# Three transformer-like blocks in one kernel: one mask in the attention, gates in other tiles, pinned table loads, kept weights fetched earlier, and copies of u on VectorE

## The chip, the core and the metric

The kernel runs on one core of a Trainium2 chip. The metric is the device time of one execution in microseconds, as the median of several runs. Five engines work side by side, each through its own list of instructions in order: TensorE (PE, matmuls and transposes), VectorE (DVE), ScalarE (ACT), GpSimd (POOL) and SyncE (SP), which here only issues DMAs. ACT issues DMAs too. An instruction that waits holds back all that stands behind it on its engine.

## The reference

Input is x of 512 tokens by 1024 channels in float32. Two hybrid layers run first, then one second block and a last RMS norm. Cut to what matters:

```
def hybrid_layer(x, ...):                      # twice
    h = rmsnorm(x, pre_mix_g)
    proj = h @ w_in                            # dn q,k,v,z,b,a; sw q,k,v; gate_a, gate_b
    y_a = deltanet_branch(...) @ w_up_dn       # causal conv, gated delta rule, norm * silu(z)
    y_b = swa_sink_branch(...) @ w_up_sw       # window 128, 16 query heads on 2 kv heads
    mix = (sigmoid(gate_a) * y_a + sigmoid(gate_b) * y_b) @ w_o
    x = x + rmsnorm(mix, post_mix_g)
    ff = square(relu(rmsnorm(x, pre_mlp_g) @ w_ff1)) @ w_ff2
    return x + rmsnorm(ff, post_mlp_g)

def second_block(x, ...):                      # once
    ua, za, ub, zb, ga, gb = split(rmsnorm(x) @ w_in_2 + b_in_2)
    # s5: dt = exp(log_dt); mag = exp(lam_re*dt); ang = lam_im*dt; bbar from b_re, b_im
    #     s_t = abar * s_(t-1) + bbar @ u_t ;  y = Re(c @ s) + d*u ; gelu, glu
    ya, yb = s5(ua) * silu(za), pool(ub) * silu(zb)
    return rmsnorm(x + (sigmoid(ga)*(ya@w_a) + sigmoid(gb)*(yb@w_b)) @ w_out)
```

In the attention a block of 128 queries sees its own block of keys and the block before it, and of each 128 of the 256 keys: those at or below the diagonal in its own block, those above it in the block before.

## The kernel before, in words

Activations lie with 128 channels on the partitions and the 512 tokens in the free dimension, so 1024 channels are eight tiles. A float32 matrix product is made of three matmuls in a rounded format: each operand is split into a high part (`xh`, `wh`) and a rest (`xl`, `wl`), and a `dense` block of 128 output channels is 8 x 3 = 24 matmuls of 128x512; `dense_half` is the same for 256 tokens. Weights come by `load_w` (L225 to L243) or by the class `Weights` (L183 to L222): SP loads a 512 KB `raw` tile, ACT casts it to the high part (L241, L221), DVE makes the rest (L242, L222). There are two `raw` tiles, three each of `wh` and `wl`, and one or two more (`rawx`, `raws`) in some stages. A tile is loaded again only when the rest of the weight in it has been made. A scheduler orders the instructions of each engine from the program; what goes through `tc.keep_in_program_order` keeps its place among its like. PSUM has 3 accumulators for the dense blocks (`psm`) and 5 others (`psa`).

The stages of a layer that the change touches, and those around them:

- **Attention.** `sw_item` (L928 to L1026) handles one block `b` of 128 queries and one of the two kv heads, 8 items a layer, beside other work. ACT makes the exponentials (L995), PE transposes the normed scores, ACT copies them to `pc` (L1007), and GpSimd cuts them: `pv` (L1010) keeps what belongs to the block before, `pc` (L1012, in place) what belongs to the own block. Then PE multiplies `pv` with the values of the block before and `pc` with those of the own block.
- **Mix stage** (L1299 to L1365). For each of eight blocks n: SP fetches `ogf` (delta-rule output) and its gate (`gate(0, n)`), DVE multiplies them (L1335), ACT and DVE split the product into `ah` parts (L336, L339), PE does the `dense` block of `w_up_sw`, and DVE multiplies the result with `gate(2, n)` (L1340). `ogf` and both gates come through `fetch` (L1313), which has three tiles (`fe`). A second loop multiplies all eight `ah` with `w_up_dn`.
- **Feed-forward stage** (L1367 to L1510). The first six blocks of `w_ff1` are done in two halves of the tokens with kept weights (`kw`); meanwhile the residual of the mix stage is finished (`rt` L432 on DVE, `xd_mid` to and from DRAM by SP, `xsl` L342). Beside it `ssm_tables` (L1047 to L1175) computes half of the tables of the second block in each layer. It loads small inputs: `row` (8x128), `dt` (64x8x1, two), `lbr`, `lbi` (64x8x16, two each), `crow` (128x2x64, four). `next(tables, None)` advances it by a step per block. The last product with `w_ff2` is done in two halves: three weights from `Weights`, then five kept ones by `load_w` (L1487). The inputs are `hh`, `hl` (relu, square, split: L1380, L1382, L336, L339); `halves3` works on the first three weights at once and leaves the last two inputs to the end.
- **State-space stage** of the second block (from L1558). `tz` tiles are read from DRAM by 32 small DMAs (L1572), 16 issued by ACT and 16 by SP. u is transposed by PE in eight groups, copied to `uab` (L1585, ACT), transposed again and copied to `u_g` (L1592, DVE), and multiplied with `e` and `tz`; ACT copies the products with `e` to `xv` (L1607).

Of the kernel before, what the change touches and what calls it, by code (L numbers as in the profile page):

```python
# [19 lines left out]
P = 128  # L20
# [34 lines left out]
def body(  # L55
# [44 lines left out]
    def rest(n):  # L100
        for _ in range(n):
            yield
# [119 lines left out]
            V.tensor_tensor(out=lo, in0=t, in1=f32(h), op=ALU.subtract)  # L222
            return h, lo

    def load_w(src, kn=KD, n=P, pool_h=False, keep=None):  # L225
        turn[0] += 1
        if turn[0] % 3 == 2 and turn[1] is not None and turn[0] > turn[2]:
            raw = turn[1].tile([P, kn, n], F32, tag="rawx", name="rawx", bufs=1)
        else:
            raw = wp.tile([P, kn, n], F32, tag="raw", name="raw", bufs=2)  # L230
        DMA.dma_start(out=raw, in_=src.rearrange("(k p) n -> p k n", p=P))
        h = lo = None
        if keep is not None:
            h, lo = keep(kn, n), keep(kn, n)
        if h is None:
            h = wp.tile([P, kn, n], F32R, tag="wh", name="wh", bufs=3)
            lo = wp.tile([P, kn, n], F32R, tag="wl", name="wl", bufs=3)
        if pool_h:
            G.tensor_scalar(out=h, in0=raw, scalar1=1.0, scalar2=0.0, op0=ALU.mult, op1=ALU.add)  # L239
        else:  # L240
            S.copy(out=h, in_=raw)  # L241
        V.tensor_tensor(out=lo, in0=raw, in1=f32(h), op=ALU.subtract)  # L242
        return h, lo  # L243

# [682 lines left out]
    def sw_item(l, b, kv, qk, vt, sw, kts, db):  # L927
# [70 lines left out]
        V.reciprocal(out=den, in_=den)  # L998
        V.tensor_tensor(out=sc, in0=sc, in1=den.unsqueeze(3).to_broadcast([P, 2, 4, P]), op=ALU.mult)
        yield from rest(PRB)  # L1000
        pcs = []
        for o in range(2):
            ps = ps_ax()
            for i in range(4):
                T.transpose(ps[:, i, :], sc[:, o, i, :], ident)
            pc, pv = sw.tile([P, 4, P], F32, tag="pc", name="pc", bufs=2), None
            S.copy(out=pc, in_=ps)  # L1007
            if b:
                pv = sw.tile([P, 4, P], F32, tag="pv", name="pv", bufs=2)
                G.affine_select(out=pv, in_=pc, pattern=[[0, 4], [-1, P]], base=0, channel_multiplier=1,  # L1010
                                compare_op=ALU.is_gt, fill=0.0)
            G.affine_select(out=pc, in_=pc, pattern=[[0, 4], [1, P]], base=0, channel_multiplier=-1,  # L1012
                            compare_op=ALU.is_ge, fill=0.0)
            pcs.append((pc, pv))
        yield from rest(PV)
        po = ps_ax()
        for o, (pc, pv) in enumerate(pcs):
            hs = slice(64 * o, 64 * o + 64)
            dst = po[hs].rearrange("p h t -> p (h t)")
            if b:  # L1020
                T.matmul(dst, lhsT=vt[:, b - 1, kv * 64:kv * 64 + 64], rhs=pv.rearrange("p h t -> p (h t)"), start=True, stop=False)
            T.matmul(dst, lhsT=vt[:, b, kv * 64:kv * 64 + 64], rhs=pc.rearrange("p h t -> p (h t)"), start=not b, stop=True)
        of = r2("sof")
        V.tensor_copy(out=of, in_=po)
        DMA.dma_start(out=db[:, 4 * kv:4 * kv + 4, b * P:(b + 1) * P], in_=of)
# [20 lines left out]
    def ssm_tables(sp, hf):  # L1046
# [6 lines left out]

        prs = slice(NG * hf, NG * hf + NG)
        grs = slice(2 * NG * hf, 2 * NG * hf + 2 * NG)
        lam = {}
        for nm, src in (("lr", ssm_lam_re_2), ("li", ssm_lam_im_2)):
            row = sp.tile([NG, P], F32, tag="row", name="row")
            DMA.dma_start(out=row, in_=src[0, grs].rearrange("(i two) p -> i (two p)", two=2))
            ps = ps_ax((P, NG))  # L1060
            T.transpose(ps, row, ident[:NG, :NG])
            lam[nm] = tl(nm)
            V.tensor_copy(out=lam[nm], in_=ps)
        lr, li = lam["lr"], lam["li"]
        dt = tl("dt")
        for half in range(2):
            DMA.dma_start(out=dt[64 * half:64 * half + 64, :],
                          in_=ssm_log_dt_2[0, grs].rearrange("(i two) -> two i", two=2)[half].partition_broadcast(64))
        bre, bim = tl("lbr", (P, NG, 2, 16))[:, :, 0, :], tl("lbi", (P, NG, 2, 16))[:, :, 0, :]
        for dst, src in ((bre, ssm_b_re_2), (bim, ssm_b_im_2)):  # L1070
            for half in range(2):
                DMA.dma_start(out=dst[64 * half:64 * half + 64],
                              in_=src[0, grs].rearrange("(i two) p c -> two p i c", two=2)[half])
        yield

# [26 lines left out]
        for src in (ssm_c_re_2, ssm_c_im_2):  # L1102
            crow = sp.tile([P, 2, 2, 64], F32, tag="crow", name="crow", bufs=2)
            for dup in range(2):
                DMA.dma_start(out=crow[:, :, dup, :], in_=src[0, grs].rearrange("(q g) c p -> (g c) q p", q=2))
            crows.append(crow)
        s16 = (P, NG, 16)
        tC, tD = tl("tC", s16), tl("tD", s16)
# [83 lines left out]
    def layer(l, st, nxt):  # L1192
# [111 lines left out]
        with sbuf(f"mx{l}") as mp:  # L1304
# [11 lines left out]
                return t  # L1316

            def gate(i, n):
                t = fetch(dg[i], n, "gate")
                if (i, n) in plain:  # L1320
                    S.activation(out=t, in_=t, func=gate_fn[i])
                return t
# [47 lines left out]
        with sbuf(f"ff{l}") as ff, ExitStack() as es2:  # L1370
# [109 lines left out]
            for i in range(2):  # L1480
                fs = Stats(tr)
                for n in range(KD):
                    if i == 0 and n == 0:
                        wk = {j: w.take() for j in range(3)}
                        head = halves3([wk[j] for j in range(3)], i)
                    elif i == 0 and n >= 3:
                        wk[n] = load_w(down(3, n)[0], keep=keep)  # L1487
                    ps = head[n] if i == 0 and n < 3 else dense_half(wk[n], hid, i)
                    ac = acc[n][:, HALVES[i]]
                    V.tensor_tensor(out=ac, in0=ps, in1=ac, op=ALU.add)  # L1490
                    fs.add(ac)
                    if i:
                        tick()

                def ff_rstd(i=i, fs=fs):
                    fm = small((P, 2), "fm")
                    V.scalar_tensor_tensor(out=fm, in0=fs.sums(), scalar=1.0 / D, in1=rs4[i], op0=ALU.mult, op1=ALU.mult)
                    V.tensor_scalar(out=fm, in0=fm, scalar1=EPS, scalar2=None, op0=ALU.add)
                    fr = power(fm, 2)
                    V.tensor_tensor(out=fr, in0=fr, in1=rs2[i], op=ALU.mult)  # L1500
                    return fr

                pending = residual(mid, acc, ff_rstd, "post_mlp", l * KD, xst, i)
                if i == 0:
                    before = pending
                    tick = ticks(before, AT_D)
# [52 lines left out]
    with sbuf("ss") as sp:  # L1559
# [20 lines left out]
        for c in range(4):  # L1580
            for j4 in range(2):
                ps = ps_ax((64, 4, P))
                for j in range(4):
                    T.transpose(ps[:, j, :], ua[:, c, 4 * j4 + j::8], ident)
                S.copy(out=uag[:, 8 * c:8 * c + 8, 4 * j4:4 * j4 + 4, :], in_=ps.rearrange("p j (g c) -> p g j c", c=16))  # L1585
        u_g = k8("u_g").rearrange("p a b -> p (a b)").rearrange("p (g b) -> p g b", g=32)
        for g8 in range(4):
            ps = ps_ax((P, 8, 64))
# [180 lines left out]
```

## Time and profile before

| | |
|---|---|
| Median of 3 runs | 2309.17 us (2308.73 to 2314.07) |
| The profiled execution | 2315.69 us, span of the trace 2313.9 us |
| Mean granted clock of TensorE | 0.982 |
| PE busy | 2243.0 us (97%) |
| DVE busy | 1485.3 us (64%) |
| ACT busy | 952.1 us (41%) |
| POOL busy | 609.4 us (26%) |
| DMA | 284.33 MB, 42% of the 16 engines' time on the main queue |

The granted clock has two levels: 1.0 is 2.4 GHz and 0.5 is 1.2 GHz. A mean between them tells which part of a stretch ran at the lower one. In the timeline a time in brackets is how long the engine sat idle before the row, and the arrow says what ended it. A row with xN stands for N like instructions; its second column is the time from the first one's start to the last one's end. SPq and ACTq are the DMA-issuing lists of SP and ACT.

### The profile page before, as it was taken

Reading aid. Unit: us, or ns where it says so; the run is one execution under the profiler, and the core shown is the slowest. Engines: PE = TensorE matmul, PEld = TensorE weight load, DVE = VectorE, ACT = ScalarE, POOL = GpSimd, SP = SyncE. Lnnn points to the kernel's source line nnn. Section 1 sums busy time; section 2 is a strip of 40 time slices with the busy share of each in tenths; the row PEclk is TensorE's granted clock in tenths of the full one; section 3 lists DMA queues with packets and bytes.
Section 4 is the critical chain, followed back from the end, with each engine's and each line's share of the span. In section 5 each row is a group of like instructions: output and inputs, shape, how many; then the busy total and the mean of one; then the engine's idle time right before and its main releaser. Section 6 shows DMA issues by size and latency. Waiting matters only on the chain. (4 is left out here: it accounts for less than half of the span.)

```text
span 2313.9 us, 37654 instructions
## 1 busy us (share of the span) xinstructions
PE 2243.0 (97%) x14460; PEld 1954.5 (84%) x14460; DVE 1485.3 (64%) x2958; ACT 952.1 (41%) x1726; POOL 609.4 (26%) x675
## 2 busy tenths in 40 slices
PE   8999999999999999999999999999999999899998
PEld 7867888887989899988678888889898898877788
DVE  5579793445576777665797934465777775435645
ACT  4554333333464354444533333334643444423333
POOL 1643420200336123246333202003351242200001
PEclk9999999999999999999999999999999999999999
DMA  5223424565453433342233345654434334563344
GB/s 177 62 72 87 101 83 128 172 200 160 121 157 92 128 107 98 116 125 58 77 87 88 92 127 182 201 164 126 136 101 118 114 97 123 169 165 117 108 131 146
DMA packets 466431, 284.33 MB, mean 123 GB/s; under 512 B 48502, under 2 KB 440012, under 8 KB 465740
## 3 DMA queue, kind: packets, MB, share of 16 engines
q1 hardware_dynamic: 462544, 280.69, 41.9%
q8 instruction: 114, 1.87, 0.3%
q10 hardware_dynamic: 3708, 1.24, 0.3%
q14 instruction: 65, 0.53, 0.1%
HBM read 235.76 MB, written 46.11 MB: 122 GB/s over the span
## 5 line engine op out<-in xcount | busy, mean ns | idle before, releaser
L78 PE MATMUL psm<-xsh,wh 128*128 128x512 f32 (+1 forms) x1136 | 445.6, 393 | 2.6 <-ACT wh L241 1.6
L78 PE MATMUL psm<-xsl,wh 128*128 128x512 f32 (+1 forms) x1136 | 432.6, 381 | 8.2 <-DVE xsl L342 4.2
L78 PE MATMUL psm<-xsh,wl 128*128 128x512 f32 (+1 forms) x1136 | 431.6, 380 | 0.0
L242 DVE TENSOR_TENSOR wl<-raw,wh 128x1024 fp32r<-128x1024 f32 (+2 forms) x179 | 213.3, 1192 | 89.9 <-ACT wh L241 63.6
L78 PEld LDWEIGHTS psm<-xsh,wh 128*128 128x128 f32 x1136 | 217.6, 192 | 48.4 <-issue 8.6
L78 PEld LDWEIGHTS psm<-xsl,wh 128*128 128x128 f32 x1136 | 218.1, 192 | 45.9 <-DVE xsl L342 5.5
L78 PEld LDWEIGHTS psm<-xsh,wl 128*128 128x128 f32 x1136 | 217.3, 191 | 40.9
L241 ACT CAST wh<-raw 128x1024 fp32r<-128x1024 f32 (+3 forms) x126 | 123.4, 980 | 253.6 <-PE psm L78 218.2
L370 POOL TENSOR_TENSOR sa<-sa,sq 128x256 f32<-128x256 f32 x54 | 51.5, 955 | 665.8 <-ACT sq L365 381.5
L78 PE MATMUL psm<-hh,wh 128*128 128x512 f32 (+1 forms) x480 | 177.1, 375 | 6.4 <-ACT hh L336 6.4
L78 PE MATMUL psm<-hl,wh 128*128 128x512 f32 (+1 forms) x480 | 177.7, 372 | 0.8 <-DVE hl L339 0.8
L78 PE MATMUL psm<-hh,wl 128*128 128x512 f32 (+1 forms) x480 | 176.7, 370 | 0.0
L221 ACT CAST wh<-raw 128x1024 fp32r<-128x1024 f32 x67 | 70.2, 1050 | 127.4 <-PE psm L78 76.2
L221 ACT CAST wh<-raws 128x1024 fp32r<-128x1024 f32 x63 | 66.0, 1047 | 127.9 <-PE psm L78 93.7
L222 DVE TENSOR_TENSOR wl<-raw,wh 128x1024 fp32r<-128x1024 f32 x67 | 97.4, 1454 | 26.0 <-ACT wh L221 23.5
L78 PEld LDWEIGHTS psm<-hh,wh 128*128 128x128 f32 x480 | 90.5, 191 | 22.8 <-ACT hh L336 7.0
L78 PEld LDWEIGHTS psm<-hl,wh 128*128 128x128 f32 x480 | 91.5, 191 | 16.4 <-DVE hl L339 1.3
L78 PEld LDWEIGHTS psm<-hh,wl 128*128 128x128 f32 x480 | 91.6, 191 | 15.1
L222 DVE TENSOR_TENSOR wl<-raws,wh 128x1024 fp32r<-128x1024 f32 x63 | 93.6, 1486 | 13.2 <-ACT wh L221 13.2
L239 POOL TENSOR_SCALAR wh<-raw 128x1024 fp32r<-128x1024 f32 (+1 forms) x53 | 62.9, 1186 | 121.0 <-PE psm L78 104.0
L78 PE MATMUL psm<-ah,wh 128*128 128x512 f32 x256 | 83.0, 405 | 5.2 <-ACT ah L336 5.0
L78 PE MATMUL psa<-xsh,wh 128*128 128x256 f32 x288 | 82.3, 286 | 0.0
(670 smaller groups left out, 5662.5 us busy)
## 6 DMA issues: line engine op xcount, KB each, us to landing
raw<-in_w_in_dram SPq DMA_DIRECT2D x130, 512.0 KB, 3.9
raw<-in_w_ff_dram SPq DMA_DIRECT2D x75, 512.0 KB, 4.1
raws<-in_w_ff_dram SPq DMA_DIRECT2D x51, 512.0 KB, 4.3
gate<-dg SPq DMA_DIRECT2D x48, 256.0 KB, 4.4
rawx<-in_w_in_dram SPq DMA_DIRECT2D x14, 512.0 KB, 4.1
raw<-in_w_up_sw_dram SPq DMA_DIRECT2D x12, 512.0 KB, 5.0
raw<-in_w_up_dn_dram SPq DMA_DIRECT2D x11, 512.0 KB, 4.5
raw<-in_w_o_dram SPq DMA_DIRECT2D x10, 512.0 KB, 4.7
```

Source lines behind the costliest of these rows:

```text
L78: return s.issue(nc.tensor.matmul(*a, **k))
L221: S.copy(out=h, in_=t)
L222: V.tensor_tensor(out=lo, in0=t, in1=f32(h), op=ALU.subtract)
L239: G.tensor_scalar(out=h, in0=raw, scalar1=1.0, scalar2=0.0, op0=ALU.mult, op1=ALU.add)
L241: S.copy(out=h, in_=raw)
L242: V.tensor_tensor(out=lo, in0=raw, in1=f32(h), op=ALU.subtract)
L370: (G if s.n in POOL_ACC else V).tensor_tensor(out=s.acc, in0=s.acc, in1=sq, op=ALU.add)
```

## The change

Five edits, in the order of the diff:

1. In the state of a kept weight, `load_w` can pin its ACT cast to program order (`pin=True`), used for two weights of the last product with `w_ff2`. These two (3 and 4) are loaded before `halves3`, and weight n + 4 is loaded in step n, so weights stand three to four blocks ahead.
2. In the attention `pc` is no longer cut. The sum p_prev v_prev + p_own v_own is formed as pc v_prev + (pc cut to the own block) (v_own - v_prev): GpSimd makes one cut (`pv`, now with the pattern of the own block), DVE makes `vd`, the difference of the values. For block 0 `pc` is used as it is.
3. The loads of `ssm_tables` go through `queue`, which pins them.
4. `gate(2, n)` goes to a `t2` tile (there are four) instead of one of the three `fe` tiles.
5. The copies to `uab` are made by DVE.

```diff
@@ load_w
-    def load_w(src, kn=KD, n=P, pool_h=False, keep=None):
+    def load_w(src, kn=KD, n=P, pool_h=False, keep=None, pin=False):
...
-            S.copy(out=h, in_=raw)
+            i = S.copy(out=h, in_=raw)
+            if pin:
+                tc.keep_in_program_order(i)
@@ sw_item
+        if b:
+            vd = sw.tile([P, 64], F32, tag="vd", name="vd", bufs=2)
+            V.tensor_tensor(out=vd, in0=vt[:, b, kv * 64:kv * 64 + 64], in1=vt[:, b - 1, kv * 64:kv * 64 + 64], op=ALU.subtract)
...
-                G.affine_select(out=pv, in_=pc, pattern=[[0, 4], [-1, P]], base=0, channel_multiplier=1,
-                                compare_op=ALU.is_gt, fill=0.0)
-            G.affine_select(out=pc, in_=pc, pattern=[[0, 4], [1, P]], base=0, channel_multiplier=-1,
-                            compare_op=ALU.is_ge, fill=0.0)
+                G.affine_select(out=pv, in_=pc, pattern=[[0, 4], [1, P]], base=0, channel_multiplier=-1,
+                                compare_op=ALU.is_ge, fill=0.0)
...
-                T.matmul(dst, lhsT=vt[:, b - 1, ...], rhs=pv..., start=True, stop=False)
-            T.matmul(dst, lhsT=vt[:, b, ...], rhs=pc..., start=not b, stop=True)
+                T.matmul(dst, lhsT=vt[:, b - 1, vs], rhs=pr, start=True, stop=False)
+                T.matmul(dst, lhsT=vd, rhs=pv.rearrange("p h t -> p (h t)"), start=False, stop=True)
+            else:
+                T.matmul(dst, lhsT=vt[:, b, vs], rhs=pr, start=True, stop=True)
@@ ssm_tables (row, dt, lbr, lbi and crow alike)
+        def queue(**k):
+            tc.keep_in_program_order(DMA.dma_start(**k))
...
-            DMA.dma_start(out=row, in_=src[0, grs].rearrange("(i two) p -> i (two p)", two=2))
+            queue(out=row, in_=src[0, grs].rearrange("(i two) p -> i (two p)", two=2))
@@ mix stage
             def gate(i, n):
-                t = fetch(dg[i], n, "gate")
+                if i == 2:
+                    t = t2("gate2")
+                    DMA.dma_start(out=t, in_=dg[i][:, n, :])
+                else:
+                    t = fetch(dg[i], n, "gate")
@@ feed-forward stage, last product
                         wk = {j: w.take() for j in range(3)}
+                        for j in (3, 4):
+                            wk[j] = load_w(down(3, j)[0], keep=keep, pin=True)
                         head = halves3([wk[j] for j in range(3)], i)
-                    elif i == 0 and n >= 3:
-                        wk[n] = load_w(down(3, n)[0], keep=keep)
+                    elif i == 0 and n + 4 < KD:
+                        wk[n + 4] = load_w(down(3, n + 4)[0], keep=keep)
@@ state-space stage
-                S.copy(out=uag[:, 8 * c:8 * c + 8, 4 * j4:4 * j4 + 4, :], in_=ps.rearrange("p j (g c) -> p g j c", c=16))
+                V.tensor_copy(out=uag[:, 8 * c:8 * c + 8, 4 * j4:4 * j4 + 4, :], in_=ps.rearrange("p j (g c) -> p g j c", c=16))
```

The edits also move instructions that the diff doesn't name, because the scheduler makes its order anew. Line numbers are those of each kernel: what was L1059, L1067, L1072 and L1105 (loads of the tables) is L1064 now, and 2 to 16 lines are added to later ones.

On SP, in the first layer's feed-forward stage, the loads of the tables stood in the middle of the residual's traffic before (`raw` are weights, `xd_mid` and `xo` the residual):

```order
L1059 DMA row<-in_ssm_lam_re_dram 8x128
L1067 DMA dt<-in_ssm_log_dt_dram 64x8x1 x2
L1072 DMA lbr<-in_ssm_b_re_dram 64x8x16
L231 DMA raw<-in_w_ff_dram 128x8x128
L1072 DMA lbr<-in_ssm_b_re_dram 64x8x16
L1072 DMA lbi<-in_ssm_b_im_dram 64x8x16
L189 DMA raw<-in_w_ff_dram 128x8x128
L1072 DMA lbi<-in_ssm_b_im_dram 64x8x16
L1105 DMA crow<-in_ssm_c_re_dram 128x2x64 x2
L1105 DMA crow<-in_ssm_c_im_dram 128x2x64 x2
L401 DMA xd_mid_5569<-rt 128x256
L430 DMA xo<-xd_in 128x256
```

Now the residual's traffic stands first and the four `crow` loads behind it, directly ahead of these rows; `tsa` and `tsb` are reads of the finished residual:

```order
L189 DMA raws<-in_w_ff_dram 128x8x128 x2
L1064 DMA row<-in_ssm_lam_re_dram 8x128
L189 DMA raw<-in_w_ff_dram 128x8x128 x3
L321 DMA tsa<-xd_mid_5565 128x512
L321 DMA tsb<-xd_mid_5565 128x512
L321 DMA tsa<-xd_mid_5565 128x512
L321 DMA tsb<-xd_mid_5565 128x512
L1064 DMA row<-in_ssm_lam_im_dram 8x128
L1064 DMA dt<-in_ssm_log_dt_dram 64x8x1 x2
L1064 DMA lbr<-in_ssm_b_re_dram 64x8x16 x2
L1064 DMA lbi<-in_ssm_b_im_dram 64x8x16 x2
L189 DMA raws<-in_w_ff_dram 128x8x128 x2
```

The small loads `dt`, `lbr` and `lbi` moved from the front of the stage, where three weight loads and the residual stood among and behind them, to a place behind five more weight loads and four of `tsa` and `tsb`; two `raws` weights stand directly behind them.

On ACT, at the first layer's last product with `w_ff2`, before (`kw` are casts of kept weights, `ft`, `fq` and `hh` make the last two inputs, `sa` and `sq` are squares for the norm):

```order
L241 CAST kw<-raw 128x1024 x2
L241 CAST kw<-rawx 128x1024
L1380 ACTIVATE ft<-y_9597 128x512
L1382 ACTIVATE fq<-ft 128x512
L336 CAST hh<-fq 128x512
L1380 ACTIVATE ft<-y_9596 128x512
L241 CAST kw<-raw 128x1024
L1382 ACTIVATE fq<-ft 128x512
L336 CAST hh<-fq 128x512
L241 CAST kw<-raw 128x1024
L365 ACTIVATE sa<-acc 128x256
L365 ACTIVATE sq<-acc 128x256 x7
```

And now:

```order
L1394 ACTIVATE ft<-y_9593 128x512
L1396 ACTIVATE fq<-ft 128x512
L1394 ACTIVATE ft<-y_9592 128x512
L338 CAST hh<-fq 128x512
L1396 ACTIVATE fq<-ft 128x512
L338 CAST hh<-fq 128x512
L241 CAST kw<-raw 128x1024 x2
L241 CAST kw<-rawx 128x1024
L367 ACTIVATE sa<-acc 128x256
L367 ACTIVATE sq<-acc 128x256 x2
L241 CAST kw<-raw 128x1024
L367 ACTIVATE sq<-acc 128x256
```

The casts of the kept weights moved behind the last `hh`. In the second layer they do so too.

On ACT, at the state-space stage, before (`za` and `p2t` are other outputs, `wh` casts of weights):

```order
L1552 ACTIVATE za<-psm,prm 128x256 x4
L1572 DMA tz<-hpad 16x8x128 x16
L1585 COPY uab<-psa 64x8x64 x5
L1535 ACT_TABLE_LOAD
L1535 ACTIVATE p2t<-psm,prm 128x512 x2
L241 CAST wh<-rawx 128x1024
L241 CAST wh<-raw 128x1024 x2
L1535 ACTIVATE p2t<-psm,prm 128x512
L1585 COPY uab<-psa 64x8x64 x3
L241 CAST wh<-rawx 128x1024
L1607 COPY xv<-psa 128x512
```

And now:

```order
L1568 ACTIVATE za<-psm,prm 128x256 x4
L1588 DMA tz<-hpad 16x8x128 x16
L1623 COPY xv<-psa 128x512 x2
L1551 ACT_TABLE_LOAD
L1551 ACTIVATE p2t<-psm,prm 128x512
L241 CAST wh<-rawx 128x1024
L1623 COPY xv<-psa 128x512 x2
L241 CAST wh<-raw 128x1024
L1551 ACTIVATE p2t<-psm,prm 128x512
L241 CAST wh<-raw 128x1024
L1551 ACTIVATE p2t<-psm,prm 128x512
```

The copies to `uab` are gone from ACT (they stand on DVE, ahead of its copy to `m8t`), and the first two copies to `xv` come directly behind the sixteen `tz` issues. On PE three dense blocks stood between the fifth and the sixth of the eight groups of u before. Now the sixth to eighth group and the second transposes stand among the first dense block, and the products with `e` and with the first `tz` tile directly behind it. Four matmuls of the second dense block later come the products with the second `tz` tile.

## Rows read from the trace of the kernel before

**Rows 1.** Waits of PE, whole span: for whom, us in total, times, longest

```profile
PE psm L78 <- ACT hh L336: 6.4, 2, 4.4
PE psa L78 <- POOL pv L1010: 6.3, 2, 3.2
PE psm L78 <- ACT ft L1380: 5.4, 2, 2.7
PE psm L78 <- ACT ah L336: 5.0, 2, 2.8
```

**Rows 2.** Windows: stretch, length, busy us and count of each engine, granted clock, DMA

```profile
125.00:145.00 20.00, 16.72 (x85) 11.05 (x83) 9.14 (x16) 13.35 (x45) 6.57 (x7) 0.91 0.17 47
1100.00:1130.00 30.00, 26.86 (x136) 19.88 (x136) 18.71 (x48) 16.52 (x50) 10.61 (x12) 0.89 0.25 71
500.00:540.00 40.00, 36.58 (x146) 29.08 (x145) 20.85 (x27) 10.58 (x13) 0.00 (x0) 0.91 0.65 197
1490.00:1520.00 30.00, 27.56 (x113) 21.87 (x112) 16.82 (x21) 8.06 (x10) 0.00 (x0) 0.94 0.69 208
620.00:660.00 40.00, 33.98 (x250) 32.95 (x250) 22.88 (x40) 22.01 (x52) 12.94 (x15) 0.91 0.62 163
1600.00:1640.00 40.00, 35.76 (x257) 34.95 (x256) 21.79 (x42) 22.41 (x53) 11.75 (x14) 0.87 0.65 171
936.00:956.00 20.00, 17.04 (x116) 16.13 (x115) 12.62 (x20) 10.40 (x16) 0.73 (x1) 0.83 0.49 141
1912.00:1932.00 20.00, 15.00 (x106) 14.30 (x105) 12.98 (x20) 11.11 (x16) 1.20 (x1) 0.83 0.55 159
2044.00:2064.00 20.00, 15.36 (x70) 11.73 (x69) 5.46 (x7) 9.90 (x15) 0.00 (x0) 0.83 0.77 168
```

**Rows 3.** Timeline of ACT, attention: start, length, row, idle before and its releaser

```profile
128.15 1.28 ACT L995 ACT_TABLE_LOAD   x1
...
132.64 1.04 ACT L1007 COPY pc<-psa 128x512 f32<-128x512 f32 x2
```

**Rows 4.** Timeline of DVE, mix stage of the first layer

```profile
499.89 0.75 DVE L1335 SCALAR_TENSOR_TENSOR ogf<-ogf,prm,gate 128x512 f32<-128x512 f32 x1 [4.48 <-DMA gate<-dg]
...
527.84 0.75 DVE L1335 SCALAR_TENSOR_TENSOR ogf<-ogf,prm,gate 128x512 f32<-128x512 f32 x1 [1.94 <-DMA gate<-dg]
```

**Rows 5.** Timeline of SP, feed-forward stage of the first layer

```profile
617.77 1.37 SPq L1067 DMA_DIRECT2D dt<-in_ssm_log_dt_dram  x2
...
621.31 0.41 SPq L231 DMA_DIRECT2D raw<-in_w_ff_dram  x1
...
630.59 2.85 SPq L1072 DMA_DIRECT2D lbi<-in_ssm_b_im_dram  x1
...
669.88 0.31 SPq L1059 DMA_DIRECT2D row<-in_ssm_lam_im_dram  x1
```

**Rows 6.** Timeline of ACT, same stage

```profile
633.02 1.04 ACT L241 CAST kw<-raw 128x1024 fp32r<-128x1024 f32 x1 [10.42 <-DMA raw<-in_w_ff_dram]
```

**Rows 7.** Line L1072, loads of lbr and lbi

```profile
DMA to landing us min/median/max: 7.9/9.7/11.5
```

**Rows 8.** Timeline of DVE, later in that stage

```profile
684.50 0.28 DVE L1030 TENSOR_TENSOR A<-cor,lbr 128x128 f32<-128x128 f32 x1
```

**Rows 9.** Timeline of ACT, last product with w_ff2, first layer

```profile
943.95 1.04 ACT L241 CAST kw<-raw 128x1024 fp32r<-128x1024 f32 x1 [1.26 <-DMA raw<-in_w_ff_dram]
```

**Rows 10.** Timeline of PE, state-space stage

```profile
2043.00 0.39 PE L78 MATMUL psm<-xsh,wh 128*128 128x512 f32 x1
...
2048.21 0.39 PE L78 MATMUL psm<-xsh,wl 128*128 128x512 f32 x1
...
2068.13 3.02 PE L78 MATMUL psa<-u_g,e 128*64 128x64 f32 x96
```

**Rows 11.** Timeline of ACT, state-space stage

```profile
2030.10 20.78 ACTq L1572 DMA_DIRECT2D tz<-hpad  x16
```

**Rows 12.** Tile tz, its loads

```profile
DMA to landing us min/median/max: 2.4/4.1/7.9
```

More of the change, by code (lines that the diff above doesn't have):

```diff
@@ L1019, in sw_item @@
             dst = po[hs].rearrange("p h t -> p (h t)")
+            pr = pc.rearrange("p h t -> p (h t)")
+            vs = slice(kv * 64, kv * 64 + 64)
             if b:
-                T.matmul(dst, lhsT=vt[:, b - 1, kv * 64:kv * 64 + 64], rhs=pv.rearrange("p h t -> p (h t)"), start=True, stop=False)
-            T.matmul(dst, lhsT=vt[:, b, kv * 64:kv * 64 + 64], rhs=pc.rearrange("p h t -> p (h t)"), start=not b, stop=True)
+                T.matmul(dst, lhsT=vt[:, b - 1, vs], rhs=pr, start=True, stop=False)
+                T.matmul(dst, lhsT=vd, rhs=pv.rearrange("p h t -> p (h t)"), start=False, stop=True)
+            else:
+                T.matmul(dst, lhsT=vt[:, b, vs], rhs=pr, start=True, stop=True)
         of = r2("sof")
@@ L1066, in ssm_tables @@
         for half in range(2):
-            DMA.dma_start(out=dt[64 * half:64 * half + 64, :],
+            queue(out=dt[64 * half:64 * half + 64, :],
                           in_=ssm_log_dt_2[0, grs].rearrange("(i two) -> two i", two=2)[half].partition_broadcast(64))
@@ L1071, in ssm_tables @@
             for half in range(2):
-                DMA.dma_start(out=dst[64 * half:64 * half + 64],
+                queue(out=dst[64 * half:64 * half + 64],
                               in_=src[0, grs].rearrange("(i two) p c -> two p i c", two=2)[half])
@@ L1104, in ssm_tables @@
             for dup in range(2):
-                DMA.dma_start(out=crow[:, :, dup, :], in_=src[0, grs].rearrange("(q g) c p -> (g c) q p", q=2))
+                queue(out=crow[:, :, dup, :], in_=src[0, grs].rearrange("(q g) c p -> (g c) q p", q=2))
             crows.append(crow)
```

## Prediction, written before the changed kernel ran

> **What bounds the kernel now.** I read the page first: PE works nearly all the span and no other engine comes near it, so only time in which PE stands still, or runs at the lower clock, can be won. The waits of PE come next. Four releasers that the change touches head its list together with residual work that it doesn't: the last `hh` parts, the cut `pv`, `ft` behind a late kept weight, and `ah` [rows 1]. Each comes twice or so, once a layer. Then I took the windows around these places for the price [rows 2]. A window shows two losses: idle time, which is its length less the busy time of PE, and the clock. At 1.2 GHz a matmul takes twice as long, so half of a stretch at that level is lost; with a mean clock c the loss is (1 - c) times the length. The reader is to see that the clock costs about as much as the waits that come before it. In us, idle and clock: attention 3.3 + 1.8 and 3.1 + 3.3; mix stage 3.4 + 3.6 and 2.4 + 1.8; start of the feed-forward stage 6.0 + 3.6 and 4.2 + 5.2; its last product 3.0 + 3.4 and 5.0 + 3.4; state-space stage 4.6 + 3.4. That is 11.5, 11.2, 19.0, 14.8 and 8.0, in all 64.5 us. More than that the change can't win, for other idle time is elsewhere.
>
> **One mask.** In the attention PE waits for the cuts of GpSimd, but these only wait for ACT: both copies to `pc` stand behind a table load and eight exponentials, from 128.15 to 132.64 [rows 3]. After the change PE's first product needs the uncut copy alone, and the first copy now stands ahead of the table load, so 4.5 us earlier; its cut is made while the exponentials run. The second copy still stands behind them, half a microsecond later than the exponentials did before, so PE still waits for it and then for its cut, which I put at 1 to 2 us a layer. What is added, twelve differences `vd` of 128x64 on DVE, has no row of its own; the nearest are small operations like the 0.28 us one on 128x128 [rows 8]. So 12 x 0.28 = 3.4 us at most and nothing below, hidden by PE's dense blocks; without that cover it costs these 3.4. I take 11.5 less 2 x 1.75 = 8, with 3 and 11.5 as ends.
>
> **Gates in other tiles.** DVE's product of `ogf` and the gate waits each time for a gate that SP could not fetch before a tile came free. From n = 3 to n = 7 this takes (527.84 - 499.89) / 4 = 7.0 us a block [rows 4], while PE needs 5.21 / 23 x 24 = 5.4 us a block [rows 10]. So the lead that the stage starts with is used up, and PE meets the last `ah` late. With `gate(2, n)` out of the three tiles, the next gate can be fetched as soon as the product before has been made: 0.75 + 4.48 and the issue, some 5.6 us a block. Over four blocks that is 5.6 us earlier, twice the wait of 2.8 [rows 1]. I take 10.5 of 11.2; ends 5 and 11.2.
>
> **Pinned table loads.** SP issues `dt` at 617.77, a kept weight in the middle of the burst at 621.31, and the last `lbi` at 630.59 [rows 5]. The weight is cast only at 633.02, after ACT has waited 10.42 us for it [rows 6]; behind that cast stands `ft`, for which PE waits, and DVE's half of the same weight stands ahead of the residual, whose late `xsl` are the second group of gaps. Now all of this comes without the burst in front. The burst is not gone: after row `lam_im`, at 669.88 before [rows 5], come `dt`, `lbr`, `lbi` and only then two weights. SP needs for it what it needed before, 630.59 - 617.77 less the two weights in between, some 12 us, and the last part lands 7.9 to 11.5 us later [rows 7]: at 690 to 693. DVE wants it at 684.50 [rows 8] and would stand for 5 to 9 us, with the rest parts of weights queued behind it. Three of these tiles exist, so a stand of about one block (5.4 us) is covered; beyond that PE waits, 0 to 3.5 us a layer and a bit of clock. I take 1.5 a layer. Two gaps of 0.6 us for the statistics stay. So 19.0 - 1.3 - 3 = 14.7; ends 6 and 18. What is late next is this DVE wait.
>
> The Trainium skill (DMA: Bandwidth & Descriptors, Anatomy of one DMA) prices a transfer at about 2.0 us plus its bytes at 436 GB/s. For the 32 KB of an `lbr` that would be an estimate of 2.1 us, by which the burst would cost nothing at either place; the trace has 7.9 to 11.5 [rows 7] and decides.
>
> **Kept weights.** At the last product ACT's order has casts of kept weights among the last `ft`, `fq`, `hh`, and one waits 1.26 us for its DMA and takes 1.04 [rows 9], in the second layer two of them. Now these casts stand behind the last `hh`, and the weights themselves are asked for earlier. What remains is DVE's `hl` and the first weights behind the three, about 1 us a layer. I take 14.8 - 2.3 = 12.5; ends 5 and 14.8.
>
> **Copies of u by VectorE.** ACT issues sixteen `tz` loads from 2030.10 for 20.78 us [rows 11] and its copies to `uab` stand behind. DVE is free there, so the wait at 2048 goes. But three dense blocks covered this time; now one does. PE gets through it, through the products with `e` (128 of them, 4.0 us [rows 10]) and the transposes of u some 2 us before the 2048.6 at which the wait of before began (two blocks less, 10.8, and some 8.5 of small work more), and then wants the second `tz` tile. Its last part is issued at about 2050.9 and lands 4.1 us later, 2.4 at least and 7.9 at most [rows 12]: at 2055, 2053.3 to 2058.8. The copies to `xv` that free PSUM for it stand behind the same issues. So PE stands some 8 us in place of two waits of 4.6 in sum, with the clock as before: 4.6 - 8 = -3.4, plus up to 1.7 of clock saved since one stop comes in place of two. I take -2; ends -8 and 8.
>
> **The sum.** 8 + 10.5 + 14.7 + 12.5 - 2 = 43.7. I take off 4 for waits that hide behind these and that the rows can't show: 40 us. The profiled execution took 2315.69 us, so 2276 on its scale. It is 6.5 us above the median of the runs, which is what is compared, so 2309 - 40 = 2269.
>
> **Rivals.**
> Handed on: each wait goes and PE meets the next late instruction, as it does with the second copy to `pc`, the `lbr` burst and `tz`. For it: three of the five parts show such a one. Against it: in the mix stage and at the last product what comes next is early. If half is kept, 20 us: 2289.
> The clock stays: the waits shrink to 1 or 2 us, but the clock still falls as often. For it: in the last product a wait of under 2 us is followed by a third of a 20 us window at 1.2 GHz [rows 2]. The clock's part of the first four is 26 us; three quarters of that kept leaves 44 - 20 = 24 off, less the 4: 2289 as well.
> The burst starves the weights: the two weights behind it come late, PE stands 8 us a layer with its clock, and the gain of part three turns into a loss: 40 - 14.7 - 16 = 9 off, 2300.
> Slower: the gates' new tiles. There are four, SP is in order, and a fetch of `gate(2, n + 4)` waits until DVE has used `gate(2, n)`. Raw weights and the other gates stand behind it. If that holds PE by d a block in the six later blocks of both layers, 12 d is lost. Without part two, 29.5 us are won, so it is slower than before beyond the measurement from d = 3 us; at the full wait for one gate, 4.48 [rows 4], it comes to 2309 - 29.5 + 54 = 2333. Against it: the fetches now stand up to four blocks ahead of their use.
> That the change doesn't do what it says, so that the waits stay: the new order shows the copies and casts where the parts need them, so I leave 1 in 50 for it, 2309.
>
> **How the numbers follow.** The forecast has 0.58, with a range of 2258 to 2282 of its own; handed on 0.18; the clock stays 0.11; starved weights 0.07; slower 0.04; no effect 0.02. The range from 2255 to 2294 holds the first three. This kernel's measurement tells about 0.3%, 7 us. Faster by more: 0.58 + 0.18 + 0.11 + most of 0.07, that is 0.91. Same: 0.05, slower: 0.04.
>
> **What would show it.** Right: no wait for `ah`, for `ft` at the burst's old place or for the last `hh` in the waits of PE; a granted clock of 1.00 in the windows of the mix stage and the last product; the cycle of the gated products at 5.4 to 5.7 us. A wait for the second `pc` or `pv` of 1 to 2 us stays, and one of 6 to 10 us for `tz` or `xv` is new at about 2046 less what was won before. Wrong: idle time of PE right after the moved burst beyond 4 us a layer, new waits for weights in the mix stage, or a clock that falls in the windows above although PE hardly waits there.

## Result and profile of the changed kernel

The changed kernel takes 2277.1 us (median of four runs, 2275.6 to 2278.8) and the kernel before 2309.6 us (four runs, 2308.7 to 2314.1). The ratio is 0.9856, interval 0.9839 to 0.9873: 1.4% or 32.5 us faster. The profiled execution of the changed kernel took 2275.63 us with a span of 2273.9 us and a mean granted clock of 0.992. Against the profiled execution of before the span is shorter by 2313.9 - 2273.9 = 40.0 us. Why 40 us in the traces are 32.5 us in the medians is the subject of the first experiment.

The waits of PE over the whole span of the changed kernel, for whom, us in total, times and longest, in the order of their size (the answer to [rows 1]):

```profile
PE psa L78 <- DMA tz<-hpad: 7.6, 1, 7.6
PE psa L78 <- POOL sa L372: 7.4, 8, 2.3
PE psm L78 <- DVE xsl L341: 7.2, 6, 2.0
...
PE psa L78 <- DVE y L312: 3.3, 2, 1.6
...
PE psm L78 <- DVE wl L244: 2.3, 4, 1.4
PE psa L81 <- DVE na L691: 2.1, 2, 1.1
...
PE psa L78 <- POOL pv L1015: 1.3, 2, 0.7
```

`hh`, `ft` and `ah` are gone from the list, and `pv` went from 6.3 to 1.3 us. New are `tz` with 7.6 us, `y` with 3.3 and `na` with 2.1: three next late instructions.

The windows at the same places of the program as in [rows 2], moved with the work; the last one is 25 us long, since the stop there takes longer:

```profile
125.00:145.00 20.00, 19.35 (x104) 14.18 (x103) 12.99 (x30) 14.39 (x49) 8.49 (x8) 1.00 0.24 67
1080.00:1110.00 30.00, 29.35 (x166) 21.58 (x165) 22.24 (x57) 17.85 (x53) 11.22 (x11) 1.00 0.25 70
488.00:528.00 40.00, 38.25 (x168) 30.91 (x167) 21.97 (x28) 10.69 (x13) 0.00 (x0) 1.00 0.67 204
1460.00:1490.00 30.00, 29.80 (x132) 24.37 (x131) 18.37 (x23) 8.17 (x10) 0.00 (x0) 1.00 0.62 187
610.00:650.00 40.00, 38.70 (x308) 37.65 (x307) 27.55 (x51) 29.21 (x68) 12.65 (x15) 1.00 0.63 180
1570.00:1610.00 40.00, 38.38 (x288) 36.26 (x287) 25.29 (x48) 27.84 (x64) 11.39 (x14) 1.00 0.67 196
915.00:935.00 20.00, 19.21 (x161) 19.04 (x160) 15.52 (x26) 13.94 (x22) 1.39 (x1) 1.00 0.54 158
1870.00:1890.00 20.00, 19.23 (x161) 19.05 (x160) 14.67 (x27) 12.91 (x22) 1.53 (x1) 1.00 0.51 149
2000.00:2025.00 25.00, 17.34 (x152) 13.59 (x149) 15.19 (x15) 6.58 (x9) 0.00 (x0) 0.80 0.72 121
```

Read as before, idle time plus (1 - clock) times the length: attention 1.3, mix stage 1.95, feed-forward stage 2.9, last product 1.6, state-space stage 7.7 + 5.0 = 12.7. In all 20.4 us, against 64.5 before: 44.1 us won here. Some 4 us of it are lost again outside these windows, where the new waits for `y` and `na` lie, 5.4 us together. The first eight windows show a clock of 1.00 throughout.

The timeline of the changed kernel where instructions moved (start, length, row, idle before and its releaser). First the attention, ACT:

```profile
126.76 0.61 ACT L1012 COPY pc<-psa 128x512 f32<-128x512 f32 x1
127.39 1.28 ACT L997 ACT_TABLE_LOAD   x1
...
131.88 0.56 ACT L1012 COPY pc<-psa 128x512 f32<-128x512 f32 x1
```

The two copies that stood together at 132.64 [rows 3] are apart now, the first ahead of the table load. Then the burst of small loads behind the row `lam_im`, by SP, ACT and DVE:

```profile
652.57 0.30 SPq L1064 DMA_DIRECT2D row<-in_ssm_lam_im_dram  x1
652.90 1.38 SPq L1064 DMA_DIRECT2D dt<-in_ssm_log_dt_dram  x2
...
655.97 6.22 SPq L1064 DMA_DIRECT2D lbi<-in_ssm_b_im_dram  x2
...
665.11 1.28 ACT L1086 ACT_TABLE_LOAD   x1 [2.92 <-DMA dt<-in_ssm_log_dt_dram]
...
666.64 0.17 DVE L1088 TENSOR_TENSOR tA<-lr,dt 128x8 f32<-128x8 f32 x1 [3.48 <-ACT dt L1086]
...
670.46 0.29 DVE L1037 TENSOR_TENSOR A<-cor,lbr 128x128 f32<-128x128 f32 x1
```

DVE stands 3.48 us, but for `dt`: ACT can go on with it at 665.11, 12.2 us after the first of its two loads was issued at 652.90. At `lbr` DVE doesn't stand at all. PE pays 60 us later, at a product that waits for DVE's `y`. The experiments show that this wait comes with the burst's new place and goes when `dt` is loaded elsewhere; by which instructions the delay is passed on was not followed:

```profile
728.56 0.48 PE L78 MATMUL psa<-tb,wh 128*128 128x256 f32 x2 [1.63 <-DVE y L312]
```

And the state-space stage, ACT and PE:

```profile
1986.78 20.97 ACTq L1588 DMA_DIRECT2D tz<-hpad  x16
...
2007.79 1.07 ACT L1623 COPY xv<-psa 128x512 f32<-128x512 f32 x2 [20.54 <-DMA tz<-hpad]
...
2011.88 1.12 PE L78 MATMUL psa<-tz,u_g 128*64 128x128 f32 x8 [7.63 <-DMA tz<-hpad]
```

The sixteen issues take 20.97 us as before [rows 11]. PE comes through to the products with the second `tz` tile at 2004.25 and stands there 7.63 us. The last of ACT's issues ends at 2007.75, 3.5 us after PE wants the tile, and the load lands 4.1 us later. Then PE runs some 10 us at 1.2 GHz.

### The profile page after: what moved, and what is told of

It reads as the page before. It is cut to its first block, busy times and chain, and to the rows that moved or that the text cites. A ratio compares the mean times of both kernels' runs of the same rounds, so it can differ in the third digit from the quotient of the medians.

```text
span 2273.9 us, 37630 instructions
## 1 busy us (share of the span) xinstructions
PE 2220.5 (98%) x14460; PEld 1938.8 (85%) x14460; DVE 1488.1 (65%) x2978; ACT 940.6 (41%) x1714; POOL 586.8 (26%) x643
## 5 line engine op out<-in xcount | busy, mean ns | idle before, releaser
L78 PE MATMUL psa<-xsl,wh 128*128 128x256 f32 x288 | 81.4, 283 | 0.0
```

Source lines behind the costliest of these rows:

```text
L78: return s.issue(nc.tensor.matmul(*a, **k))
```

## Experiments

Theory: the five parts act each at its own place, so their gains add up; the kernel before has a clock that varies from one execution to the next, and its profiled one was unlucky; the copies of u by VectorE gain nothing, since PE runs into the late `tz`. Rival for each: named in its expectation.

**The kernel before, profiled once more.** No edit.

> The kernel before, once more, for a second profile. Why: the trace of the changed kernel is 40 us shorter than the first trace of before, as the sum had it, but the medians differ by only 32.5 us, because the first trace of before was 6.5 us above its median. Theory: that trace was unlucky at the very places the change touches, so a trace near 2309 us shows a smaller sum of idle time and clock loss in the nine windows of the prediction than 64.5 us, about 58. Rival: the 6.5 us lie elsewhere, spread over the matmuls, and the nine windows again lose 64 to 65 us.

It took 2308.44 us, with a span of 2306.6 and a clock of 0.987. Its windows at the mix stage and at the start of the feed-forward stage, each in the first and the second layer:

```profile
500.00:540.00 40.00, 37.34 (x163) 30.00 (x161) 22.28 (x29) 11.48 (x15) 0.00 (x0) 1.00 0.70 215
1490.00:1520.00 30.00, 27.33 (x118) 22.10 (x119) 17.99 (x23) 8.58 (x11) 0.00 (x0) 1.00 0.70 213
620.00:660.00 40.00, 33.89 (x259) 32.62 (x258) 21.92 (x41) 24.24 (x57) 10.95 (x13) 0.96 0.68 181
1600.00:1640.00 40.00, 34.38 (x235) 32.36 (x233) 23.99 (x44) 26.78 (x62) 10.21 (x12) 0.91 0.71 193
```

Over all nine places the idle time is 35.9 us (35.1 in the first trace [rows 2]), but the clock costs 19.0 us and not 29.5. In the mix stage PE stood nearly as long as in the first trace, 5.3 us against 5.9, and the clock did not fall at all. So the first trace of before lost 10.5 us more to the lower clock than this one, at almost the same idle time. The kernel's clock does vary: in 45 more executions its mean lay between 0.982 and 0.990 and the time between 2306.8 and 2319.2 us. The time of the first trace lay 6 us above the median and the changed kernel's profiled time 1.5 us below its own: these 7.5 us are the difference between 40 and 32.5.

**The change without the copies by VectorE.**

```
-                V.tensor_copy(out=uag[...], in_=ps...)
+                S.copy(out=uag[...], in_=ps...)
```

> The changed kernel with the copies to uab given back to ACT. In the changed kernel PE waits 7.63 us for the second tz tile and runs 10.24 us at the lower clock after it: 12.7 us in that window against 8.0 before. Theory: the copies on DVE only let PE run ahead into the tz loads, so this part costs 4.7 us; without it 2272 us (2269 to 2275), with the old wait for uab of about 3 us back and no wait for tz. Rival (the copies do help, and the tz wait comes from the other parts): 2280 us or more, with both waits.

Measured 2269.8 us, ratio 0.9824 (0.9809 to 0.984), inside the theory's range. Its waits in that stage are those of before, 3.2 us for `uab` and 0.8 for a weight, and no `tz`; its window there:

```profile
1996.00:2021.00 25.00, 21.05 (x131) 16.32 (x131) 7.13 (x10) 11.80 (x18) 0.00 (x0) 0.80 0.85 161
```

Idle 3.95 us against 7.66 in the changed kernel, at the same loss of clock: 3.7 us in this window, 7.3 us between the medians, whose intervals leave room for both. The spans of the two traces differ by 7.2 us, but the rest of that lies far from the edit: some 2 us of clock between 100 and 200 us and 1.8 us of idle time between 500 and 600, which the changed kernel's trace has and this one hasn't.

**The copies by VectorE alone**, the same two lines the other way round in the kernel before.

> The kernel before with only the copies to uab moved to DVE. Theory: the wait for uab (3.0 us) and the wait for wh (1.4 us) go, one for tz of 7 to 8 us comes: 2309 + 4.7 = 2314 us (2311 to 2317). Rival: the part gains what the window lost, 4 to 8 us: 2302 to 2306 us.

Measured 2312.3 us, ratio 1.0005 (0.9996 to 1.0014): 1.2 us slower, nothing that can be told from no change, and the rival's gain is excluded. The largest stop in that stage, and its window:

```profile
PE psa L78 <- ACT wh L241: 7.0, 1, 7.0
```

```profile
2036.00:2061.00 25.00, 17.99 (x173) 14.21 (x168) 15.27 (x15) 6.58 (x9) 0.00 (x0) 0.80 0.66 120
```

Two waits of 4.4 us in sum became one of 7.0, and the clock costs 5.0 us here, where before it cost 3.4. The instruction that stands is the theory's, the products with the second `tz` tile at 2047.81. The profile names another releaser for it, a cast by ACT that ends at 2047.71, behind the same sixteen issues. That is some 4 us lost in the window, where the medians show 1.2; as in the second experiment, window and medians agree only to some 3 us.

**The `tz` tiles laid out beforehand.** The changed kernel, with the eight shifted copies of `hpad` written to DRAM as one array when the tables are made, so that a `tz` tile is one load and ACT issues two DMAs instead of sixteen.

```
+    d_tz = dp.tile([P, 32, P], F32, name="d_tz")
...
+        for j in range(8):
+            DMA.dma_start(out=d_tz[16 * j:16 * j + 16, grs], in_=hpad[:, grs, (7 - j) * 16:(7 - j) * 16 + 128])
...
-            for j in range(8):
-                (S if g8 < 2 else DMA).dma_start(out=tz[16 * j:16 * j + 16], in_=hpad[...])
+            (S if g8 < 2 else DMA).dma_start(out=tz, in_=d_tz[:, 8 * g8:8 * g8 + 8, :])
```

> The changed kernel with the tz tiles laid out in DRAM in their final form during the feed-forward stages (8 DRAM to DRAM copies at the end of the tables in each layer), so that the state-space stage loads each tile with one DMA of 512 KB in place of eight. Theory (the 16 issues of 21 us on ACT are what PE waits for, directly for tz and through the copies to xv behind them): the wait for tz goes or falls under 2 us and the clock stays up: 2277 - 10 to 12.7 = 2264 to 2268 us. Rival (landing and traffic, not the issues, set the time): a wait of 5 us or more stays, 2273 us or more. Second rival: the 16 copies delay weights in the feed-forward stages and give the gain back: 2275 us or more with new waits there.

Measured 2264.0 us, ratio 0.9794 (0.978 to 0.9808). ACT's issues and the window of the stage:

```profile
1988.32 0.84 ACTq L1590 DMA_DIRECT2D tz<-d_tz  x2
```

```profile
2000.00:2025.00 25.00, 24.52 (x226) 19.78 (x226) 22.56 (x22) 9.34 (x13) 0.00 (x0) 1.00 0.41 140
```

20.97 us of issues are 0.84, PE stands half a microsecond and the clock stays at 2.4 GHz: 12.2 us won in the window, 13.1 between the medians. The laid-out form removes the long list of issues and the late landing of the last load together, so this run doesn't part the two.

**The same with the copies of u by ACT**, as in the second experiment.

> The tz tiles ready in DRAM as in e4, and the copies to uab by ACT as in the kernel before. Theory (the sixteen issues in front were the whole matter, who copies is not): no wait for uab and none for tz, 2264 us like e4 (2261 to 2268). Rival (the copies on DVE are worth something by themselves): a wait for uab or wh of 2 us or more stays, 2268 us or more.

Measured 2262.8 us, ratio 0.9798 (0.9784 to 0.9812), equal to the one before. With the small loads out of the way it makes no difference that can be measured who copies. This and the one before are the fastest kernels of the study, 2% faster than before.

**Four parts, each alone in the kernel before.** The mask:

```
+            vd = sw.tile([P, 64], F32, tag="vd", name="vd", bufs=2)
+            V.tensor_tensor(out=vd, in0=vt[:, b, ...], in1=vt[:, b - 1, ...], op=ALU.subtract)
...
+                T.matmul(dst, lhsT=vt[:, b - 1, vs], rhs=pr, start=True, stop=False)
+                T.matmul(dst, lhsT=vd, rhs=pv..., start=False, stop=True)
```

> The kernel before with the one mask alone. In two traces of before the attention windows lose 11.5 and 10.0 us, in the changed kernel 1.3. Theory (a wait removed is a wait won): 9.4 us won, less 2.1 if the new waits for na of 1.05 us a layer come from this part: about 0.3 to 0.4% faster, 2301 to 2303 beside a before of 2310; the trace shows whether the waits for na are there. Rival (gaps are handed on): under 5 us, with new waits of PE in the rest of the attention.

The gates:

```
-                t = fetch(dg[i], n, "gate")
+                if i == 2:
+                    t = t2("gate2")
+                    DMA.dma_start(out=t, in_=dg[i][:, n, :])
```

> The kernel before with the gates in other tiles alone. The mix windows lose 11.2 us in the first and 5.3 in the second trace of before (the clock fell in one and not in the other), 1.9 in the changed kernel. Theory: 3.4 to 9.3 us won, about 6, 0.27%; no waits for ah, the gated products 5.4 to 5.7 us apart. Rival: the lead gained in the stage is lost at its end or at the start of the next one, under 2 us.

The table loads:

```
+        def queue(**k):
+            tc.keep_in_program_order(DMA.dma_start(**k))
...
-            DMA.dma_start(out=dt[64 * half:64 * half + 64, :],
+            queue(out=dt[64 * half:64 * half + 64, :],
```

> The kernel before with the pinned table loads alone. The windows lose 19.0 and 16.9 us in the two traces of before, 2.9 in the changed kernel: 15 us won there. New in the changed kernel are waits of PE for y of 1.63 us in each layer's feed-forward stage. Theory: these come from this part, because the dt load, now behind the row, lands later, and the operations of GpSimd on the tables with it (3.3 us later against the row): 12 us won, 0.5%, 2298, with the waits for y in the trace. Rival: the waits for y come from elsewhere (the residual, now early): 15 us won, 2295, no waits for y.

The kept weights:

```
+                        for j in (3, 4):
+                            wk[j] = load_w(down(3, j)[0], keep=keep, pin=True)
...
+                    elif i == 0 and n + 4 < KD:
+                        wk[n + 4] = load_w(down(3, n + 4)[0], keep=keep)
```

> The kernel before with the kept weights three blocks ahead alone. The windows lose 14.8 and 15.4 us in two traces of before, 1.6 in the changed kernel. Theory: 13.5 us won, 0.58%, 2296 to 2298, no wait for hh. Rival: half, 7 us, because the residual behind it (its waits for xsl and sa at the end of the layer) takes up the lead.

| part | us | ratio | gain, us | interval of the gain | forecast |
|---|---|---|---|---|---|
| one mask | 2304.3 | 0.9969 | 7.2 | 4.2 to 10.4 | 8 |
| gates | 2305.5 | 0.9974 | 6.0 | 3.7 to 8.1 | 10.5 |
| table loads | 2299.6 | 0.9949 | 11.8 | 8.6 to 14.8 | 14.7 |
| kept weights | 2298.9 | 0.9940 | 13.9 | 10.4 to 17.3 | 12.5 |
| copies of u (third experiment) | 2312.3 | 1.0005 | -1.2 | -3.2 to 0.9 | -2 |

The gains are one less the ratio, times 2312. The first four make 38.9 us alone; all four together, without the copies, made 2311 x (1 - 0.9824) = 40.7. They add up, within their intervals. Each took its own wait off the list, and two brought their new ones along: `na` 2.1 us with the mask alone, `y` with the table loads alone, where ACT again stands for `dt`:

```profile
PE psa L78 <- DVE y L310: 3.2, 2, 1.6
```

```profile
672.26 1.28 ACT L1079 ACT_TABLE_LOAD   x1 [3.21 <-DMA dt<-in_ssm_log_dt_dram]
```

**`dt` by ACT, earlier.** The kernel with the laid-out `tz`, its two loads of `dt` issued by ACT and not pinned:

```
-            queue(out=dt[64 * half:64 * half + 64, :],
+            S.dma_start(out=dt[64 * half:64 * half + 64, :],
```

> As e4, with the two dt loads issued by ACT instead of SP; they stand then at the start of the feed-forward stage between the squares and the casts of kept weights. In the first trace of before the DMA engines moved nothing for some 9 us after these loads were issued by SP, and the weight behind them landed 11.7 us after its issue. Theory (a): what stops is SP's own row of transfers, ACT's can go on beside it: dt is early, no waits for y (1.63 us a layer), and no new waits at the kept weights: 2264 - 3 = 2261 us. Rival (b): the DMA engines themselves are held for 9 us: the kept weight and ft are late again, the waits of PE for ft are back, 2270 us or more.

Measured 2277.4 us, ratio 0.9856 (0.984 to 0.9873): 13 us of what was won is gone, as the rival said. Some 11 of them are lost at 600 to 640 and 1560 to 1600 us, where idle time and clock together cost 13.7 us here and 2.9 in the kernel with the laid-out `tz`. The loads now stand at 611.10 and 612.37. The busy share of the DMA engines in tenths, and what they move, in 40 slices of 608 to 630 us; then the packets of ACT's queue in this stretch, ACT's timeline and PE's wait:

```profile
DMA  9998100000000000000000000144899995100004
GB/s 365 384 374 292 56 0 0 0 0 0 0 0 0 0 0 0 0 0 0 0 0 0 0 0 0 14 76 116 235 323 348 326 263 177 33 11 16 0 9 105
...
q10 hardware_dynamic: 1056, 0.00, 2.1%
```

```profile
611.10 0.70 ACTq L1078 DMA_DIRECT2D dt<-in_ssm_log_dt_dram  x1
...
626.02 1.05 ACT L241 CAST kw<-raw 128x1024 fp32r<-128x1024 f32 x1 [10.78 <-DMA raw<-in_w_ff_dram]
```

```profile
PE psm L78 <- ACT ft L1397: 6.8, 2, 3.4
```

A slice is 0.55 us: for twenty of them, 610.75 to 621.75, the rate is 0 GB/s. In the first five SP had asked for nothing; its weight of 512 KB issued at 613.61 then waits some 8 us for its first bytes. From 614 to 621 us all 677 packets are ACT's, about 97 a microsecond, and the 16 engines are busy 5% of the time. So the loads hold up not only the list that they stand in but what SP has issued too; by what means the trace doesn't show. The wait for `y` is gone and the one for `ft` of before [rows 1] is back. The Trainium skill (DMA: Bandwidth & Descriptors, Issuing engines are not separate DMA queues) says that DMAs run on the same 16 DMA engines whichever engine started them. This trace agrees in that ACT's loads delay SP's.

**`dt` once at the start**, for both halves into a constant tile:

```
+    dtc = cst.tile([P, 16], F32, name="dtc")
...
+            S.dma_start(out=dtc[64 * half:64 * half + 64, :], in_=ssm_log_dt_2[0]...partition_broadcast(64))
```

> As e4, with dt for both layers loaded once into a constant tile by two DMAs that ACT issues at the very start. Theory: the waits for y are gone in both layers (3.3 us) and the operations on the tables in GpSimd's list run some 3 us earlier against the row; at the start, where PE waits for the input rows and grow anyway, the loads cost 0 to 2 us: 2261 to 2264. Rival: they hold the first weights and rows for up to 9 us: 2268 to 2273, with longer waits in the first 30 us.

Measured 2272.8 us, ratio 0.9836 (0.9823 to 0.985), the rival's range, 9 us above the kernel with the laid-out `tz`. The first 30 us of this kernel, and then of that one:

```profile
0.00:30.00 30.00, 11.38 (x41) 8.85 (x42) 10.18 (x22) 10.21 (x19) 5.25 (x16) 1.00 0.43 126
```

```profile
0.00:30.00 30.00, 19.19 (x108) 16.77 (x109) 18.58 (x36) 16.31 (x31) 6.96 (x17) 0.94 0.60 191
```

PE works 7.8 us less there, against which that kernel loses 1.8 us by its clock of 0.94, and the DMA engines move 126 instead of 191 GB/s. What the loads delay now are the input rows, for which ACT waits, and the first weights behind them:

```profile
11.86 1.06 ACT L466 ACTIVATE xn<-xrow 128x1024 f32<-128x1024 f32 x1 [4.80 <-DMA xrow<-in_x_dram]
```

The waits for `y` are gone, which gives 3.3 us back. That accounts for 2.7 of the 9 us; where the rest is lost was not found. A place for these loads in a stretch where the DMA engines have little to do was not tried, nor a form of `dt` in DRAM that is not read in pieces of 4 bytes.

## Why the prediction was right, and where its sizes were off

**The time.** 2269 was forecast, the median is 2277, inside the likeliest case's own range. The sum itself is met to the tenth in the traces, 40.0 us of span, but that is luck: in the windows of the two traces its terms came to 10.2, 9.3, 16.1, 13.2 and -4.7 us for 8, 10.5, 14.7, 12.5 and -2, and the errors cancel; the 4 us taken off for hidden waits came to 4.1. What failed is its last step, "which is what is compared, so 2309 - 40 = 2269": the profiled execution was known to be 6.5 us above the median, and the 40 us were nevertheless taken off the median in full. The second trace of before shows where the excess lay: in the very windows that the sum was made of, as clock. What an unlucky execution lost there can be won only on its own scale. With the clock of the second trace, 54.9 - 20.4 = 34.5 us are to be won in the windows, 30 after the 4 us lost outside them; the medians say 32.5.

**One mask.** Right: 7.2 us alone for 8. The wait for the second `pv` is 0.7 us a layer, smaller than "1 to 2 us". That PE now meets `na` of DVE, 2.1 us in this part alone as in the whole, was not foreseen; with the 1.3 us for `pv` it comes to 3.4, which by luck is near the 3.5 that the forecast put aside for `pv` alone.

**Gates.** The wait for `ah` is gone, the gain of 6.0 is below 10.5. Part of this is the clock once more: the second trace of before shows 5.3 us to be won here in place of 11.2. The cycle of the gated products is longer than the 5.4 to 5.7 us forecast:

```profile
493.05 0.75 DVE L1349 SCALAR_TENSOR_TENSOR ogf<-ogf,prm,gate 128x512 f32<-128x512 f32 x1 [4.51 <-DMA gate<-dg]
...
505.75 0.75 DVE L1349 SCALAR_TENSOR_TENSOR ogf<-ogf,prm,gate 128x512 f32<-128x512 f32 x1 [3.42 <-DMA gate<-dg]
506.42 1.22 DVE L244 TENSOR_TENSOR wl<-raw,wh 128x1024 fp32r<-128x1024 f32 x1
...
517.29 0.75 DVE L1349 SCALAR_TENSOR_TENSOR ogf<-ogf,prm,gate 128x512 f32<-128x512 f32 x1 [3.67 <-DMA gate<-dg]
```

That is (517.29 - 493.05) / 4 = 6.06 us, and DVE still waits each time for a gate. The lead of the stage's start now lasts to its end, which is all that PE needs. The 2 us that the two windows still lose are three waits for the low part of a weight, the longest of them 1.4 us (`wl` in the list above), at 507.69. This isn't the rival that the new tiles hold SP and its weights up: DVE makes that part only at 506.42, behind a product that waited 3.42 us for its gate, while ACT had cast the weight some 6 us before.

**Table loads.** The mechanism held in the main: the wait goes, the burst comes later, DVE stands behind it, and PE pays. Two details were wrong. DVE waits for `dt`, which is issued first and is there 12.2 us later, and not for `lbr`; and it stands 3.5 us, not 5 to 9. PE pays not there, but at `y` in 728.56, so the cover of three tiles did hold. That it pays 1.6 us a layer where 1.5 were put is thus luck, for the 1.5 stood for a wait behind `lbr` that didn't come. The estimate of 2.1 us for an `lbr` that stands beside the forecast uses a fit of the Trainium skill (DMA: Bandwidth & Descriptors, Anatomy of one DMA) that the page gives for DMAs issued by GpSimd; these are SP's. Alone it gave 11.8 for 14.7, an interval that just takes in the forecast; the clock's share may again be the difference, since the second trace has 16.9 us here in place of 19.0.

**Kept weights.** Right, 13.9 alone for 12.5; no wait for `hh` is left, and the clock stays at 1.00.

**Copies of u.** The chain of events came as written: PE through to the second `tz`, a stop of 7.63 us (forecast 8), `xv` behind the same issues. The step "plus up to 1.7 of clock saved since one stop comes in place of two" had the wrong sign: the clock's loss went from 3.4 to 5.0 us. Alone it cost 1.2 us for the 2 forecast, within an interval that holds no change too; on top of the other parts it cost 3.7 us in the window and 7.3 between the medians. The kernels with the laid-out `tz` show the cause: with the small loads gone both forms of the copy take the same time.

**Rivals.** The clock stays: it did not, eight of nine windows stand at 1.00. Handed on: in three places, as `tz`, `y` and `na`, 13 us in sum, but mostly where the forecast had put it. Starved weights: no; the two weights behind the burst made no wait that shows in the list of PE. Slower by the gates' new tiles: no, that part alone won 6.0 us.

## What to carry to other kernels

Where a profiled execution is above the median, ask in which term the excess sits, and take a term made of it off on the profile's scale only: a loss by the clock is one that a second trace may not show. A long list of small DMA issues on a computing engine delays every instruction behind it; moving one of these to another engine only uncovered the next here, while laying the data out once, so that a load is one DMA, removed them all. And a burst that holds up the other transfers had a cost at each of the four places where these runs have it, so look for the place where the fewest wait.

## What the runs showed of the hardware

- While two loads of 2 KB were under way, each of 512 pieces of 4 bytes spread over 64 partitions, next to nothing else moved on the 16 DMA engines. When ACT issued them alone, a weight that SP issued at 613.61 had its first bytes only at 621.75. In the changed kernel, where SP issues them and `lbr` and `lbi` follow, the rate is 0 GB/s for 8.3 us. A weight behind the first of these loads landed 11.7 us after its issue in the kernel before; which property of the loads does it was not tried. It isn't always a full stop: with `dt` loaded at the start, in twice as many such pieces, nothing else moved from 6 to 8 us, but 87 GB/s did from 17 to 22 us, beside 93 pieces a microsecond. The changed kernel, 40 slices of 650 to 672 us, `dt` issued at 652.90:

```profile
GB/s 253 346 179 123 264 339 229 39 0 0 0 0 0 0 0 0 0 0 0 0 0 0 0 14 50 38 91 59 99 216 309 342 345 308 241 69 3 0 0 0
```

- The same kernel with nearly the same idle time, 35.1 and 35.9 us, lost 29.5 us to the lower clock in one execution and 19.0 in another, in the same nine windows. In the mix stage windows with 3.4 and 2.4 us of idle time had a fall in the one, and windows with 2.7 and 2.7 us had none in the other. Why is not settled by these runs.
- Sixteen DMA issues of 64 KB on ACT took 19.3 to 21.0 us in nine traces, two of 512 KB took 0.84 us in four.
